# Work from two head pairs on stands in where a head pair's own steps would wait, in the second mixer of a streaming encoder

## The chip, the cores and the metric

The kernel runs on one core of one Trainium2 chip. The metric is the device time of one execution in microseconds (us). A core has five engines with a queue of instructions each, and each works its queue strictly in order: PE (TensorE, matmuls; its weight loads are listed apart as PEld), DVE (VectorE), ACT (ScalarE), POOL (GpSimd) and SP (SyncE, which here only issues DMAs). An instruction that waits for another engine holds up all that stands behind it in its own queue.

## The reference

One inference step of two layers for 1,152 tokens (1,024 of a prompt and 8 streams of 16), with a model width of 1,024. Layer 0 is stick-breaking attention beside a convolution; layer 1 is a banded attention with a learned bias by relative position; each is followed by a squared-ReLU MLP. The change lies in layer 1's mixer:

```python
def c_project(h, w_in):
    B, T, _ = h.shape
    p = (h @ w_in).reshape(B, T, 3, N_C_HEADS, HEAD_DIM)
    return p[:, :, 0], p[:, :, 1], p[:, :, 2]

def band_attention(q, k, v, q_pos, k_pos, rel_bias):
    s = jnp.einsum('bqhd,bkhd->bhqk', q, k).astype(jnp.float32) * (HEAD_DIM ** -0.5)
    rel = jnp.clip(q_pos[:, None] - k_pos[None, :], -REL_CLIP, REL_CLIP) + REL_CLIP
    s = s + rel_bias[:, rel].astype(jnp.float32)
    ...
    p = jax.nn.softmax(jnp.where(mask, s, -jnp.inf), axis=-1)
    return jnp.einsum('bhqk,bkhd->bqhd', p.astype(v.dtype), v)
```

Sixteen heads of 64 are computed; every token sees its own chunk of 64 and the eight chunks before it, with a running cache for the streams.

## The kernel before

All is in 32-bit floats; a factor is split into a high and a low part (`split`, lines 183 to 186: ACT copies the high part, DVE subtracts to get the low one), and a product is three matmuls of them.

**The second mixer** (`mixer1`) goes through eight pairs of heads, p = 0 to 7. For one pair it needs three projections, q, k and v (chunks 3p, 3p + 1 and 3p + 2 of the weights), each for three groups g of 384 tokens. One such sum, of one chunk and one group, is 24 matmuls (`dense`, line 225), which come as two steps of 12; the text calls 12 such matmuls a *block*. A pair has 18 blocks. Their result is in a PSUM bank `psc{p}{n}{g}` (n is 0 for q, 1 for k, 2 for v) until DVE scales it into `sq`, `sk` or `sv` (line 1122). The weights of a chunk come in two halves `hl_wc{chunk}_{half}`: SP loads them to a `st` buffer (three of them), then ACT and DVE split them into one of four `hl` buffers, so that two chunks fit.

The attention of pair p has two heads i and, for each, four jobs t of two query tiles q of 128. A tile's chain is: scores on PE (`zc{p}{i}{q}`, lines 1201 and 1202), the bias and the maximum on DVE (line 1165, in two parts where the tile is wide), the exponential on ACT (line 1168), the scaling on DVE (lines 1169 and 1170) into `s{p}{i}{q}`. For a job, PE then turns the blocks of its two tiles (`tpc{p}{i}{t}{group}`, line 455), ACT and DVE split them (`whc`, `wlc`), PE multiplies with the values (`avc{p}{i}{t}`, line 467), and ACT and DVE finish (`atc`, `cpc`). Beside it run the streams' tokens (`zs`, `zn`, `sn`, `st`, `so`, `sq{p}{bg}`). Before a pair begins, `expand_qk` makes its `q`, `k` and `l` operands on ACT and DVE (lines 348 to 353), and they overwrite those of the pair before.

**What sets the order.** The work of a pair is three lists of steps: `steps` (the attention, with what is carried over from the pair before), `sample` (the streams) and `fill` (the projections of the next pair, 18 blocks). `merge` (lines 53 to 76) lays them into one. It keeps a clock of PE's planned time; a step has a planned PE cost and may have to come a lag after a named step. Among the heads of the lists it takes the one that is ready first, and among those ready the one whose list is least far on. The merged order goes to a framework that queues each engine's instructions and may still let one slip past another on the same engine where it expects a wait. From pair 1 to pair 6 the `fill` list runs out before `steps` does, because the last job's turns and products follow each other with lags. The last job of pair p (i = 1, t = 3) is carried into pair p + 1. Pair 7 has the output projection (`psoa`) as its `fill` and loads `cr` from memory for it. Here *tail of pair p* is the stretch from `tpc{p}12` on, where PE has only steps left that hang on each other.

Of the kernel before, what the change touches and what calls it, by code (L numbers as in the profile page):

```python
# [49 lines left out]
        self.pe, self.go, self.dve, self.name, self.after, self.lag = pe, go, dve, name, after, lag  # L50


def merge(*lists):


    lists = [steps for steps in lists if steps]
    total = [sum(s.pe for s in steps) or 1.0 for steps in lists]
    at, done = [0] * len(lists), [0.0] * len(lists)
    out, now = [], 0.0
    ends = {s.name: 1e9 for steps in lists for s in steps if s.name}  # L60
    while True:
        heads = []
        for n, steps in enumerate(lists):
            if at[n] < len(steps):
                s = steps[at[n]]
                ready = max(now, ends.get(s.after, -1e9) + s.lag)
                heads.append((ready, (done[n] + 0.5 * s.pe) / total[n], n, s))
        if not heads:
            return out
        now, _, n, s = min(heads, key=lambda e: e[:3])  # L70
        out.append(s)
        at[n] += 1
        done[n] += s.pe
        now += s.pe
        if s.name:
            ends[s.name] = now
# [22 lines left out]
def run(steps):  # L99
    for s in steps:  # L100
        s.go()
# [23 lines left out]
def tile_trunk(ctx, tc, ins, outs):  # L125
# [128 lines left out]
    def new_hs(name):  # L254
        return [[new_h(g, half, name) for half in range(2)] for g in range(NG)]
# [54 lines left out]
    def chunk_steps(n, got, ahead, h, ks, evac, name, depth=1, per=12):  # L310

        steps = [Step(0.0, lambda: [ahead(n + d) for d in range(depth + 1)], 1200.0)]
        for g in range(NG):
            box = {}

            def ps(g=g, box=box):
                if "p" not in box:
                    box["p"] = bank(f"ps{name}{g}")
                return box["p"]

            steps += dense(ps, lambda: got[n], h, g, ks, per)
            steps.append(Step(0.0, lambda g=g, ps=ps: evac(ps(), g), 470.0))
        return steps

    def chunks_steps(ns, got, ahead, h, ks, evac, name, depth=1):

        steps = [Step(0.0, lambda: [ahead(n) for n in range(ns[0], ns[-1] + depth + 1)])]
        for g in range(NG):
            for n in ns:
                box = {}  # L330

                def ps(g=g, n=n, box=box):
                    if "p" not in box:
                        box["p"] = bank(f"ps{name}{n}{g}")
                    return box["p"]

                steps += dense(ps, lambda n=n: got[n], h, g, ks)
                steps.append(Step(0.0, lambda n=n, g=g, ps=ps: evac(n, ps(), g), 470.0))
        return steps
# [757 lines left out]
    def mixer1(nx, win):  # L1097
        h, rstd = nx.h, nx.r
        with ExitStack() as st:
# [12 lines left out]
            def staged(p, n, ps, g):  # L1112
                tag = ("sq", "sk", "sv")[n]
                if p == 0 and n < 2:
                    if n == 0:
                        nx.run_rows(g)
                    elif g == 0:
                        nx.end(1)
                        nx.end(2)
                if g == 0:  # L1120
                    S[tag, p] = pp.tile([P, T], F32, tag, f"{tag}1{p}")
                tt(S[tag, p][:, g * G:g * G + G], ps[:, :G], rstd[g], ALU.mult)
                if g == 2 and n:
                    put(outs["c_k" if n == 1 else "c_v"][p], S[tag, p])

            def proj(p):
                if p == 0:
                    return (chunks_steps([0, 1], got, ahead, h, ks, lambda n, ps, g: staged(0, n, ps, g), "c")
                            + [Step(0.0, lambda: expand_qk(0))]
                            + chunk_steps(2, got, ahead, h, ks, lambda ps, g: staged(0, 2, ps, g), "c02"))  # L1130
                steps = []
                for n in range(3):
                    steps += chunk_steps(3 * p + n, got, ahead, h, ks, lambda ps, g, n=n: staged(p, n, ps, g),
                                         f"c{p}{n}")
                return steps

            def expand_qk(p):
                q, k = S["sq", p], S["sk", p]
                expand(qs, kd, kl, q, k)
                S["qn"] = pp.tile([P, P], F32, "qn", f"qn1{p}")  # L1140
                S["kn"] = pp.tile([P, P], F32, "kn", f"kn1{p}")
                ACT(S["qn"], q[:, TP:], AF.Copy, scale=0.125)
                ACT(S["kn"], k[:, TP:], AF.Copy)
# [43 lines left out]
            def attend(p, cat):  # L1187
                def job(i, t):
                    ws = {}

                    def one(q):
                        n = min(q + 1, 5) * P
                        k0 = (q + 1) * P - n
                        b0 = 640 - n
                        s = ep.tile([P, 640], F32, "s", f"s{p}{i}{q}")
                        pieces = []
                        qc = slice(q * P, q * P + P)
                        for c, m in ((0, n),) if n <= 512 else ((0, 384), (384, 256)):
                            z = bank(f"zc{p}{i}{q}{c}")
                            kc = slice(k0 + c, k0 + c + m)  # L1200
                            mm(z[:, :m], qs[i][:, qc], kd[i][:, kc], start=True, stop=False)  # L1201
                            mm(z[:, :m], qs[i][:, qc], kl[i][:, kc], start=False, stop=True)  # L1202
                            pieces.append((z[:, :m], S["bp", p, i][:, b0 + c:b0 + c + m], c, m))
                        softmax(s, pieces, n, f"c{p}{i}{q}")
                        ws[q] = (s, k0)

                    q0, q1 = 2 * t, 2 * t + 1
                    keys = {j: [q for q in (q0, q1) if max(0, q - 4) <= j <= q] for j in range(max(0, q0 - 4), q1 + 1)}
                    blocks = Blocks(keys, lambda j, q: ws[q][0][:, j * P - ws[q][1]:j * P - ws[q][1] + P])

                    def cost(q):
                        return 2 * max(256, min(q + 1, 5) * P) * PASS

                    name = f"c{p}{i}{t}"
                    return (Step(cost(q0), lambda: one(q0), 1100.0), Step(cost(q1), lambda: one(q1), 1100.0, f"z{name}"),
                            split_weigh_steps(vs, wk, cat, i, t, blocks, name, f"z{name}"))

                return [job(i, t) for i in range(2) for t in range(4)]
# [6 lines left out]
                s["w"] = w  # L1225

            run(proj(0))
            carry, cat_t = [], None
            for p in range(8):
                S["p"] = p  # L1230
                if p == 7:
                    cat_t = new_hs("cat1")
                cat = Cat(1, p, wk, cat_t)
                jobs = attend(p, cat)
                s3 = jobs[3][0]
                s3.go = lambda p=p, go=s3.go: (bias_p(p, 1), go())
                body, left = pipeline(jobs[1:], jobs[0][2])
                steps = carry + [jobs[0][0]]
                steps += [Step(327.0, lambda p=p, g=g: expand_v(p, g)) for g in range(NG)]
                if p == 7:  # L1240
                    bias_p(p, 0)
                    expand_qk(p)
                    run(merge(steps, ready_chunks(1, range(3), pp, cat_t)))
                    steps = []
                steps += [jobs[0][1]] + body
                carry = left
                cs = sample_out(cat, wk, p)
                sample = [Step(0.0, lambda p=p: biases(p))]
                load = sample_caches(1, p, cp)
                sample += two_samples(*(sample_steps(1, p, bg, S, wk, load, soft, cs) for bg in range(2)))  # L1250
                back = []
                if p < 7:
                    fill = proj(p + 1)
                else:
                    fill = sum(part_out(1, range(3), pp, cat_t), [])
                    steps += carry
                    back = ready_chunks(1, range(3, 7), pp, cat_t)
                if p < 7:
                    bias_p(p, 0)
                    if p:  # L1260
                        expand_qk(p)
                run(merge(steps, sample, fill, back))
            return cat_t


# [701 lines left out]
```

## Time and profile before

| | us |
|---|---|
| median of three runs | 2751.92 |
| lowest and highest of them | 2749.00, 2752.41 |
| the profiled execution's own time | 2750.03 |
| its span, first to last instruction | 2748.2 |

The profile is of one execution. Its rows give a start in us from the span's start, a duration, the engine, the line, the operation, output<-inputs with the buffers' numbers left out, a count (x12) and, in brackets, the idle time of the engine before it and what ended that. Matmuls overlap each other, so a row of x12 lasts longer than its share of PE's time; the weight loads (PEld) keep step with it. The "releaser" of a wait is inferred. Most of the kernel is outside `mixer1`: its eight pairs take from about 1,333 to 1,946 us.

### The profile page before, as it was taken

What the parts mean: (1) busy time and instruction counts of PE and PEld (TensorE: products, weight loads), DVE (VectorE), ACT (ScalarE), POOL (GpSimd) and SP (SyncE); (2) the same over time, 40 slices, a digit from 0 to 9 for tenths busy, and PEclk for the clock granted to TensorE, in tenths of its full rate; (3) what the DMA queues carried; (4) which work ended last, traced back from release to release, by engine and by line L of the source; (5) the groups of instructions that cost most, each with busy time, mean ns of one, the idle gap of its engine ahead of it and who ended that gap; (6) DMA issues with size and microseconds to landing.
All of it is one profiled execution on the core that took longest, in us unless ns stands there. A gap on an engine that the chain in (4) does not pass through costs nothing.

```text
span 2748.2 us, 50583 instructions
## 1 busy us (share of the span) xinstructions
PE 2669.0 (97%) x19362; PEld 2557.1 (93%) x19362; DVE 2090.5 (76%) x4117; ACT 1389.0 (51%) x2906; POOL 328.3 (12%) x599
## 2 busy tenths in 40 slices
PE   8999898999999999999999999998999999999998
PEld 8987776799999999999999999997999999999998
DVE  8999998888777755758577777778787777647577
ACT  5344456755554543435355555556555555434344
POOL 1100101041111100000011111110221111100001
PEclk9999999999999999999999999999999999999999
DMA  4434446454343377435444444446533343684344
GB/s 157 121 111 147 118 141 223 145 176 143 139 146 141 138 260 250 124 100 170 146 140 138 140 135 135 139 132 229 179 132 137 141 145 138 230 270 134 96 125 145
DMA packets 173203, 422.90 MB, mean 154 GB/s; under 512 B 25968, under 2 KB 53808, under 8 KB 170912
## 3 DMA queue, kind: packets, MB, share of 16 engines
q1 hardware_dynamic: 135696, 288.38, 33.1%
q0 software_dynamic: 37120, 131.27, 13.9%
q8 instruction: 152, 2.49, 0.4%
q14 instruction: 91, 0.75, 0.1%
q10 hardware_dynamic: 144, 0.02, 0.0%
HBM read 289.60 MB, written 117.34 MB: 148 GB/s over the span
## 4 chain that ended last, share of the span: by engine, by line
PE 76%; DVE 12%; ACT 4%; issue 4%; DMA 3%; POOL 0%; SPq 0%; DVEq 0%; ACTq 0%; POOLq 0%
PE um L1461 25%; PE pd L1686 25%; PE psc L225 10%; PE psp L225 3%; DVE y L735 3%; PE avc L467 2%; PE tpc L455 2%; DVE kp L907 2%; PE f L225 1%; PE psoa L225 1%; DMA cr<-cat_d 1%; PE zc L1201 1%; PE zc L1202 1%; PE zs L568 1%; PE so L602 1%
## 5 line engine op out<-in xcount | busy, mean ns | idle before, releaser
L225 PE MATMUL psc<-h,hl_wc 128*128 128x384 f32 x1728 | 327.2, 339 | 0.0
L225 PEld LDWEIGHTS psc<-h,hl_wc 128*128 128x128 f32 x1728 | 296.8, 188 | 13.3 <-issue 10.9
L1461 PE MATMUL um<-sl,hl_m 128*128 128x288 f32 x1548 | 240.3, 295 | 0.0
L1461 PEld LDWEIGHTS um<-sl,hl_m 128*128 128x128 f32 x1548 | 217.7, 188 | 0.0
L1686 PE MATMUL pd<-tm,hl_wd 128*128 128x288 f32 x1584 | 214.7, 294 | 0.0
L1686 PEld LDWEIGHTS pd<-tm,hl_wd 128*128 128x128 f32 x1584 | 211.3, 189 | 0.0
L735 DVE SCALAR_TENSOR_TENSOR y<-u,dw,y 128x1024 f32<-128x1024 f32 (+1 forms) x232 | 177.8, 806 | 0.6
L225 PE MATMUL psp<-h,hl_wi 128*128 128x384 f32 x864 | 165.7, 344 | 0.0
L1468 ACT ACTIVATE hdm<-hdm 128x288 f32<-128x288 f32 x192 | 84.7, 442 | 156.5 <-DVE hdm L1467 154.8
L225 PEld LDWEIGHTS psp<-h,hl_wi 128*128 128x128 f32 x864 | 150.9, 191 | 7.0 <-issue 6.2
L186 DVE TENSOR_TENSOR tm<-xr,tm 128x576 fp32r<-128x576 f32 (+1 forms) x120 | 85.8, 715 | 93.9 <-ACT tm L185 93.6
L185 ACT ACTIVATE tm<-xr 128x576 fp32r<-128x576 f32 (+1 forms) x120 | 77.6, 646 | 95.8 <-PE pd L1686 74.0
L1168 ACT ACTIVATE s<-s,mxc 128x640 f32<-128x640 f32 (+4 forms) x128 | 88.9, 694 | 60.2 <-DVE mxc L1165 58.6
L1461 PE MATMUL um<-sl,hl 128*128 128x288 f32 x756 | 119.1, 296 | 0.0
L1686 PE MATMUL pd<-th,hl_wd 128*128 128x288 f32 x792 | 113.7, 297 | 3.8 <-DVE th L186 3.7
L1686 PEld LDWEIGHTS pd<-th,hl_wd 128*128 128x128 f32 x792 | 108.2, 190 | 4.8 <-DVE th L186 4.2
L1686 PE MATMUL pd<-xr,hl_wd 128*128 128x288 f32 x792 | 112.4, 296 | 0.0
L1686 PEld LDWEIGHTS pd<-xr,hl_wd 128*128 128x128 f32 x792 | 108.0, 190 | 0.0
L1461 PEld LDWEIGHTS um<-sl,hl 128*128 128x128 f32 x756 | 106.4, 188 | 0.8
L1686 PE MATMUL pd<-tm,hl 128*128 128x288 f32 x768 | 104.9, 295 | 0.0
L1686 PEld LDWEIGHTS pd<-tm,hl 128*128 128x128 f32 x768 | 103.1, 188 | 0.0
L185 ACT ACTIVATE whc<-tpc 128x512 fp32r<-128x512 f32 (+1 forms) x144 | 72.5, 523 | 46.7 <-PE tpc L455 45.8
(526 smaller groups left out, 6637.0 us busy)
## 6 DMA issues: line engine op xcount, KB each, us to landing
xr<-hb_d SPq DMA_DIRECT2D x208, 288.0 KB, 3.0
xr<-in_w_up_dram SPq DMA_DIRECT2D x64, 512.0 KB, 4.2
hb_d<-hdm POOLq DMA_DIRECT2D x96, 288.0 KB, 2.4
hb_d<-t POOLq DMA_DIRECT2D x96, 288.0 KB, 2.4
wm<-in_w_down_dram SPq DMA_DIRECT2D x64, 256.0 KB, 4.0
st_wd<-in_w_down_dram SPq DMA_DIRECT2D x64, 256.0 KB, 3.5
st_wc<-in_w_in_c_dram SPq DMA_DIRECT2D x44, 256.0 KB, 2.9
xm_d<-xo POOLq DMA_DIRECT2D x16, 576.0 KB, 3.5
```

The source lines that it names most:

```text
L185: ACT(hi, src, AF.Copy)
L186: return tt(lo, src, f(hi), ALU.subtract)
L225: mm(ps()[:, :G], hl[:, a, at:at + P], act[g][k // 4][b][:, k % 4, :], start=n == 0, stop=n == len(todo) - 1)
L455: nc.tensor.transpose(tp[:, c0 + q * P:c0 + (q + 1) * P], blocks.get(j, tile_q), ident)
L467: mm(st["av"][:, o0:o0 + n], vs[:, j, i].rearrange("p a d -> p (a d)"), src[:, c0:c0 + n], start=st["done"] == 0, stop=st["done"] == nmm - 1)
L568: mm(box["z"][at // 512][own, at % 512:at % 512 + kw], qb[:, own], k[:, b * kw:b * kw + kw], start=True, stop=True)
L735: stt(src if j == CW - 1 else dst, src, wj, dst, ALU.mult, ALU.add)
L907: nc.vector.tensor_tensor_scan(keep[:, 0:n][:, ::-1], keep[:, 0:n][:, ::-1], ones[:, 0:1].to_broadcast([P, n]), 1.0, ALU.mult, ALU.mult)
L1168: ACT(s[:, :n], s[:, :n], AF.Exp, bias=mx, scale=-1.0, accum_out=tot)
L1461: mm(banks[b, n][:, :TQ], w[:, a, c * P:c * P + P], combo(key, c)[:, h, n * TQ:n * TQ + TQ], start=k < 3 and c == 0 and i == 0, stop=c == ...
L1468: ACT(y, y, AF.Relu)
L1686: mm(ps, w[:, a, m * P:m * P + P], b[:, h, (n - ns[0]) * TQ:(n - ns[0]) * TQ + TQ], start=first and s == 0, stop=j == NJ - 1 and s == 2, s ...
```

## The change

`merge` takes one more list, `spare`. Where the earliest head of all lists is still more than 400 ns of planned time away, it puts the next step of `spare` there instead. `mixer1` gives it, for pairs 0 to 5, the first three steps of the projections two pairs on: loading ahead, and the two blocks of `psc{p+2}00`. What was not placed leads the next pair's `fill`, and what was placed is missing from it.

```diff
-def merge(*lists):
+def merge(*lists, spare=()):
...
         if not heads:
             return out
+        if spare and min(heads)[0] > now + 400.0:
+            out.append(spare.pop(0))
+            now += out[-1].pe
+            continue
         now, _, n, s = min(heads, key=lambda e: e[:3])
...
-            carry, cat_t = [], None
+            carry, cat_t, left_over, rest_of = [], None, [], []
...
                 back = []
+                spare = []
                 if p < 7:
-                    fill = proj(p + 1)
+
+                    fill, spare = left_over + (rest_of if p else proj(1)), []
+                    if p < 6:
+                        rest_of = proj(p + 2)
+                        spare, rest_of = rest_of[:3], rest_of[3:]
...
-                run(merge(steps, sample, fill, back))
+                run(merge(steps, sample, fill, back, spare=spare))
+                left_over = spare
```

No instruction of the eight pairs is added or taken away; they change places. In pairs 0 and 1 PE's `fill` still has 18 blocks. Pair 0 places none of its spare. In pairs 1 to 5 both spare blocks are placed, so that the `fill` of pairs 2 to 6 has 16 blocks, and those of pairs 2 to 5 get two more at their tails. Pair 6 has no spare: 16 blocks in all, against 18 before. Counted by pair, two blocks move from each pair 2 to 6 to the one ahead of it; the sum is that pair 1 has two more and pair 6 two fewer. Lines of the changed kernel are up to ten higher (225 is 229, 455 is 459, 467 is 471, 1201 is 1205).

Three places carry the prediction. The first is PE at the tail of pair 1: `sq111` is the last thing before the wait for `whc1120`. Before, with "..." for the rest of the scores and for turns:

```order
L610 MATMUL sq111_16213<-ident_69,sb111_16081 128x128
L467 MATMUL avc112_16220<-whc1120_16200,vs1_14196 128x256 x2
L1201 MATMUL zc1170_16226<-k1_14193,q1_14191 128x384
...
L467 MATMUL avc112_16220<-wlc1120_16201,vs1_14196 128x256 x2
...
L467 MATMUL avc112_16220<-whc1121_16209,vs1_14196 128x256 x2
L467 MATMUL avc112_16220<-wlc1121_16210,vs1_14196 128x256 x2
L455 MATMUL tpc1130_16298<-ident_69,s116_16168 128x128
L225 MATMUL psc300_16307<-h1_00_13863,hl_wc9_0_15924 128x384
```

In the changed kernel, with "..." for the rest of a block (the first) and for scores, turns and products (the second):

```order
L614 MATMUL sq111_16213<-ident_69,sb111_16081 128x128
L229 MATMUL psc300_16230<-h1_00_13863,hl_wc9_0_15924 128x384
...
L229 MATMUL psc300_16230<-h1_30_13975,hl_wc9_0_15924 128x384
L471 MATMUL avc112_16243<-whc1120_16200,vs1_14196 128x256 x2
L471 MATMUL avc112_16243<-wlc1120_16201,vs1_14196 128x256 x2
L1205 MATMUL zc1170_16249<-k1_14193,q1_14191 128x384
...
L471 MATMUL avc112_16243<-wlc1121_16210,vs1_14196 128x256 x2
L229 MATMUL psc300_16230<-h1_40_13712,hl_wc9_1_15929 128x384
```

The first block of `psc300` now stands ahead of the products of `whc1120`, and the second whole behind those of `wlc1121`; before, `psc300` came in pieces behind the first turn of `s116`, 15 of its matmuls ahead of the first turn of `s117`. Now 24 are.

The second is ACT at the tail of pair 2 (pairs 3 to 5 read alike), where PE waits for `whc2120`. Before:

```order
L1168 ACTIVATE s216_17073,totc216_17084<-s216_17073,mxc2161_17082 128x640
L185 ACTIVATE hl_wc13_1_17198<-st_wc13_1_17196 128x512
L185 ACTIVATE whc2120_17105<-tpc2120_17100 128x512
L185 ACTIVATE whc2121_17114<-tpc2121_17109 128x512
L348 ACTIVATE k1_14193<-sk13_16664 64x1024
```

In the changed kernel:

```order
L1172 ACTIVATE s216_17115,totc216_17126<-s216_17115,mxc2161_17124 128x640
L189 ACTIVATE whc2120_17147<-tpc2120_17142 128x512
L189 ACTIVATE whc2121_17156<-tpc2121_17151 128x512
L352 ACTIVATE k1_14193<-sk13_16552 64x1024
L189 ACTIVATE whc2122_17183<-tpc2122_17180 128x256
```

The split of the next weights no longer stands between the exponential of `s216` and `whc2120`. PE's order there has 12 matmuls of `psc400` ahead of `avc211` and 12 ahead of `tpc2120`, where those of `psc322` were, and 19 of `psc401` between `tpc2120` and the turns of `s217`, where 15 of `psc400` were. `sq121` has moved ahead of the first of these.

The third is the tail of pair 6. PE before, with "..." for the rest of a block and for products and scores:

```order
L1202 MATMUL zc615384_20644<-l1_14195,q1_14191 128x256
L225 MATMUL psc722_20656<-h1_00_13863,hl_wc23_0_20139 128x384
...
L225 MATMUL psc722_20656<-h1_30_13975,hl_wc23_0_20139 128x384
L467 MATMUL avc611_20669<-whc6110_20628,vs1_14196 128x256 x2
...
L1202 MATMUL zc616384_20687<-l1_14195,q1_14191 128x256
L225 MATMUL psc722_20656<-h1_40_13712,hl_wc23_1_20144 128x384
...
L225 MATMUL psc722_20656<-h1_70_13826,hl_wc23_1_20144 128x384
L455 MATMUL tpc6120_20710<-ident_69,s614_20608 128x128
L455 MATMUL tpc6120_20710<-ident_69,s615_20640 128x128
```

PE in the changed kernel, with "..." for the rest of the products and scores:

```order
L1206 MATMUL zc615384_20670<-l1_14195,q1_14191 128x256
L614 MATMUL sq161_20681<-ident_69,sb161_20559 128x128
L471 MATMUL avc611_20688<-whc6110_20654,vs1_14196 128x256 x2
L1205 MATMUL zc6160_20703<-k1_14193,q1_14191 128x384
L1206 MATMUL zc6160_20703<-l1_14195,q1_14191 128x384
L471 MATMUL avc611_20688<-wlc6110_20655,vs1_14196 128x256 x2
...
L1206 MATMUL zc616384_20706<-l1_14195,q1_14191 128x256
L459 MATMUL tpc6120_20717<-ident_69,s614_20634 128x128
L459 MATMUL tpc6121_20726<-ident_69,s614_20634 128x128
L459 MATMUL tpc6120_20717<-ident_69,s615_20666 128x128
```

And DVE in the changed kernel at the same place, from the first part of `s615`'s maximum to its scaling, with "..." for small steps of 128x1 ("ISA" is the bias with the maximum; lines 1174, 642 and 481 are 1170, 638 and 477 of the kernel before):

```order
L1169 ISA s615_20666,mxc6150_20673<-zc6150_20667,bp61_20292 128x384
...
L642 COPY cs16_20425<-sq161_20681 64x64
L1174 TENSOR_SCALAR s614_20634<-s614_20634,totc614_20645 128x640
L1169 ISA s615_20666,mxc6151_20675<-zc615384_20670,bp61_20292,mxc6150_20673 128x256
...
L642 COPY cs16_20425<-sq161_20681 64x64
L481 TENSOR_TENSOR cpc611_20699<-avc611_20688,atc611_20697 64x256
L1169 ISA s616_20702,mxc6160_20709<-zc6160_20703,bp61_20292 128x384
...
L1169 ISA s616_20702,mxc6161_20711<-zc616384_20706,bp61_20292,mxc6160_20709 128x256
...
L1174 TENSOR_SCALAR s615_20666<-s615_20666,totc615_20677 128x640
```

Both blocks of `psc722` are gone from here (they stand ahead of `avc610` now), so that `zc615`, `avc611`, `zc616` and the turns of `s614` and `s615` follow each other directly. On DVE the first two parts for `s616` and two copies for `sq161` now come ahead of the scaling of `s615`; before, that scaling was ahead of `s616`.

## The prediction

> **What bounds the kernel now.** The page comes first, for the bound of the whole; then PE's waits in the second mixer; then its tails in order of time.
>
> ```profile
> span 2748.2 us, 50583 instructions
> PE 2669.0 (97%) x19362; PEld 2557.1 (93%) x19362; DVE 2090.5 (76%) x4117; ACT 1389.0 (51%) x2906; POOL 328.3 (12%) x599
> ```
>
> PE is busy in 97% of the span, so a change of order can win idle time of PE and nothing else: 79 us in the whole kernel. Asked for PE's waits from 1430 to 1850 us (pair 0 to the last of pair 6's body), the trace lists two (columns: total, times, longest):
>
> ```profile
> PE avc L467 <- ACT whc L185: 5.7, 5, 1.2
> PE tpc L455 <- DVE s L1170: 2.5, 6, 0.7
> ```
>
> The five and the six are the tails of pairs 1 to 5 (and one of pair 0); in the bodies between them PE waits for nothing. The windows show the pairs one by one (length, busy time of PE, PEld, DVE, ACT, POOL, granted clock, DMA):
>
> ```profile
> 1506.90:1577.02 70.12, 68.56 (x506) 64.58 (x505) 51.76 (x146) 38.04 (x89) 8.97 (x22) 1.00 0.45 137
> 1787.43:1857.57 70.14, 68.56 (x505) 64.59 (x505) 51.41 (x145) 37.48 (x87) 8.86 (x21) 1.00 0.44 132
> 1857.57:1865.10 7.53, 3.14 (x21) 2.65 (x20) 6.91 (x15) 5.52 (x11) 2.19 (x4) 0.92 0.63 181
> 1865.10:1871.00 5.90, 5.75 (x27) 5.35 (x28) 3.51 (x7) 2.91 (x6) 0.82 (x3) 0.53 0.99 267
> ```
>
> The pairs repeat to 0.02 us: 70.1 us, of which PE idles 1.6. So all that the five tails can give is about 5 x 1.5 = 7.5 us, 0.27% of the span. The third row is pair 6's tail, where PE works 3.1 us of 7.5; in the fourth PE runs at a clock of 0.53.
>
> The tail of pair 1, in order of time:
>
> ```profile
> 1503.57 2.04 PEld L225 LDWEIGHTS psc<-h,hl_wc 128*128 128x128 f32 x12
> 1505.93 0.83 ACT L1168 ACTIVATE s<-s,mxc 128x640 f32<-128x640 f32 x1 [1.73 <-DVE mxc L1165]
> 1506.63 0.27 PE L610 MATMUL sq<-ident,sb 128*128 128x128 f32 x1
> 1506.76 0.61 ACT L185 ACTIVATE hl_wc<-st_wc 128x512 fp32r<-128x512 f32 x1
> 1507.40 1.09 ACT L185 ACTIVATE whc<-tpc 128x512 fp32r<-128x512 f32 x2
> 1508.05 0.51 PE L467 MATMUL avc<-whc,vs 128*128 128x256 f32 x2 [1.14 <-ACT whc L185]
> 1508.06 1.29 DVE L186 TENSOR_TENSOR wlc<-tpc,whc 128x512 fp32r<-128x512 f32 x2
> 1509.06 1.06 ACT L348 ACTIVATE k<-sk 64x1024 fp32r<-64x1024 f32 x1 [0.57 <-PE zc L1201]
> 1511.63 0.83 ACT L1168 ACTIVATE s<-s,mxc 128x640 f32<-128x640 f32 x1
> 1513.44 0.55 DVE L1170 TENSOR_SCALAR s<-s,totc 128x640 f32<-128x640 f32 x1
> 1514.05 0.88 PE L455 MATMUL tpc<-ident,s 128*128 128x128 f32 x6 [0.36 <-DVE s L1170]
> ```
>
> Two waits are to be seen: 1.14 us for `whc1120`, which ACT begins only after an exponential and a split of weights, and 0.36 us for `s117`. A block of 12 matmuls takes 2.04 us, 0.17 us each; it is longer than either wait.
>
> **The change, part by part.** No instruction is added; the terms are the waits at six tails.
>
> *Pair 1* gets two blocks that it did not have. The first starts at 1506.90 where PE stopped, and ends at 1508.94, after `whc1120` came (1508.05): the wait of 1.14 goes. By the turns of `s117` PE has now done 24 matmuls of `psc300`, not 15, so it arrives 9 x 0.17 = 1.5 us of work later. `s117` itself moves little: `zc117` ends about 1.1 us later, but its exponential now stands ahead of `q1` on ACT, and the scaling that ended at 1513.99 comes at about 1513.6 to 1514.2. PE's own work to there is the first block's 2.04, the second's 2.04 and the 3.0 us of small matmuls that lie between 1508.05 and 1513.69 beside 15 x 0.17: arrival at about 1514.0. Both waits go: **-1.5 us** (bounds 0, if `s117` slips by as much as its scores, and -1.5).
>
> *Pairs 2 to 5* have the same count of blocks as before, from other chunks. What differs is, on ACT, the 0.61 us split that no longer stands ahead of `whc`: `whc` can start when the exponential ends (1505.93 + 0.83 and a small read, about 1506.9), takes 0.55, and PE goes on at about 1507.5, not 1508.05. Ahead of `s217` stand 19 matmuls and not 15, 4 x 0.17 = 0.7 us that cover the 0.36. On the other side DVE now does `q1` (1.22 us, in the rows below) ahead of the scaling, which takes back what DVE gained from the earlier `whc`. So the turns of `s217` start at the old time, with 0.7 us more of PE's work behind them, less a short new wait for `whc2122`, which now stands ahead of more fill: **-0.5 us each, -2.0 in all** (bounds -1.5 and +0.5 each).
>
> *Pair 6* loses two blocks, 2 x 2.04 = 4.1 us of work. If PE's work bound this tail, it would be 4.1 us shorter, and the term would cancel what pair 1 took on. But it hangs on DVE:
>
> ```profile
> 1850.90 1.15 DVE L186 TENSOR_TENSOR wlc<-tpc,whc 128x512 fp32r<-128x512 f32 x2
> 1851.96 0.55 DVE L1165 CUSTOM_DVE_ANT_0 s<-zc,bp 128x384 f32<-128x384 f32 x1
> 1852.66 0.48 DVE L1165 CUSTOM_DVE_ANT_0 s<-zc,bp,mxc 128x256 f32<-128x256 f32 x1
> 1854.35 2.24 PE L225 MATMUL psc<-h,hl_wc 128*128 128x384 f32 x12
> 1854.59 0.56 DVE L1170 TENSOR_SCALAR s<-s,totc 128x640 f32<-128x640 f32 x1
> 1855.18 0.42 DVE L477 TENSOR_TENSOR cpc<-avc,atc 64x256 f32<-64x256 f32 x1
> 1856.43 1.03 PE L455 MATMUL tpc<-ident,s 128*128 128x128 f32 x8
> 1858.46 0.51 PE L467 MATMUL avc<-whc,vs 128*128 128x256 f32 x2 [0.89 <-ACT whc L185]
> 1859.09 0.21 DVE L638 COPY cs<-sq 64x64 f32<-64x64 f32 x1
> 1860.33 0.56 DVE L1165 CUSTOM_DVE_ANT_0 s<-zc,bp 128x384 f32<-128x384 f32 x1
> 1861.83 1.22 DVE L351 TENSOR_TENSOR l<-sk,k 64x1024 fp32r<-64x1024 f32 x1
> 1863.28 1.22 DVE L353 SCALAR_TENSOR_TENSOR q<-sq,q 64x1024 fp32r<-64x1024 f32 x1
> 1864.53 0.55 DVE L1170 TENSOR_SCALAR s<-s,totc 128x640 f32<-128x640 f32 x1
> 1865.14 1.54 PE L455 MATMUL tpc<-ident,s 128*128 128x128 f32 x6 [3.25 <-DVE s L1170]
> ```
>
> In the new order DVE does, from the end of the `wlc` at 1852.05: first part of `s615` 0.55, scaling of `s614` 0.55, second part 0.48, two copies 0.42, `cpc611` 0.42, the two parts of `s616` 0.55 and 0.48, scaling of `s615` 0.56, and some 0.3 of reciprocals: 4.3 us, `s615` at 1856.4. PE, without the blocks, is at these turns 4.1 us before 1856.43 and waits some 3.5 to 4 us in a new place. From there the gain is small: four turns (half of the row of x8, 0.5 us) and one `whc` (0.55 to 0.6) put `avc612` at about 1857.6 instead of 1858.46, and DVE then has `wlc` twice, the parts of `s617`, `l`, `q`, `wlc`, `cpc` and the scaling, the same as before. The end at 1865.14 comes 0.9 us earlier. Of the 4.1 us of work taken out, 3.2 stay as waiting: **+3.2 us** (bounds +1.0, if DVE follows more closely, and +4.1).
>
> *The clock at pair 6.* In the old trace one wait of 3.25 us was followed by a granted clock of 0.53 for 5.9 us, while waits of 1.14 left it at 1.00. The new wait for `s615` is 3.5 to 4, so I let the clock fall there too. It then lies on the chain: six turns take 1.54 us and not 0.88 (both rows above), and products and scores up to `zc617` lose about 0.5 as well: **+1.2 us** (bounds 0 and 2.7, the latter for PE's 5.75 busy us at 0.53). [...] The trace has a drop after 3.25 us already, so here it takes no longer wait than that.
>
> *Queues.* On SP the bias of the next pair (`bp30` and so on) moves behind two loads of weights, some 30 us ahead of use: nothing. At the start of pair 7 `cr` loads move ahead of a bias; PE's idle time there is 74.00 - 69.63 = 4.4 us in this row:
>
> ```profile
> 1871.00:1945.00 74.00, 69.63 (x497) 63.23 (x496) 61.63 (x182) 42.87 (x109) 4.30 (x8) 1.00 0.60 206
> ```
>
> No step there has a clear side: 0, bounds -1 and +1.
>
> **Sum.** -1.5 - 2.0 + 3.2 + 1.2 = +0.9 us. The profiled execution took 2750.03 us and would take 2750.9; it lies 1.9 below the median of the runs, 2751.92, so the forecast against the median is 2752.8. A measurement of this kernel can tell about 0.2% from no change, 5.5 us: 2746.4 to 2757.4. That is no change.
>
> **The rivals.**
>
> *All five tails lose their waits and pair 6 follows* (faster). For it: in pairs 2 to 5 a split leaves ACT's queue and more fill stands in the second wait. Against it: these pairs get no block more than before. It gives -1.5 for pair 1, -6.0 for the four others, +1.5 for pair 6 with the clock as before: -6.0, so 2745.9. It decides where PE idles under 0.3 us at the tails of pairs 2 to 5. Chance 0.08.
>
> *Pair 6 loses its cover and its clock* (slower). Mechanism: the wait for `s615` trips the clock, PE is too idle after it to get it back, and it stays at half through the wait for `s617` into pair 7. For it: the row at 0.53 after 3.25 us, and 3.1 busy us in the 7.5 before that. Against it: the stretch hangs on DVE and ACT, which keep their speed. It costs the whole cover of 4.1, 1.2 on the chain and 2.7 for a second stretch like that row; with pair 1's -1.5 and nothing from pairs 2 to 5 that is +6.5, so 2758.4. It decides if the clock stays under 0.6 for over 10 us around pair 6's tail. [...] Chance 0.12.
>
> *It does not do what it says*: at pairs 2 to 5 the spare only stands in for the block that is missing from the same place, pair 1's second wait comes back behind the longer fill, and pair 6's tail shortens as PE's work does. Each term is near 0: 2751.9. Chance 0.10.
>
> **How the numbers follow.** The forecast has 0.70, 2752.8. Same is 0.70 + 0.10 = 0.80, faster 0.08, slower 0.12. The range takes pairs 2 to 5 at -1.2 each and pair 6 at +1.0 without the clock term for its low end (-1.5 - 4.8 + 1.0 = -5.3, which leaves the faster rival out), and the slower rival at the other (+6.5); drawn in by 0.8 and 0.5, since not all bounds come together: 2747.4 to 2757.9.
>
> **What would show it.** Right: the window of pair 1's tail has no wait of PE over 0.3 us; those of pairs 2 to 5 keep one for `whc` of 0.5 to 0.9; at pair 6 a new wait of PE for DVE's scaling of 3 us or more stands ahead of `tpc6120`'s turns, with a clock under 0.7 behind it; the bodies of pairs 2 to 6 stay free of waits. Wrong: a period of pairs 2 to 5 that differs from 70.1 by over 1 us, new waits in a body (fewer blocks between scores and turns), or a pair 6 that is 4 us shorter than before.

## The result, and the profile after

| | before | after |
|---|---|---|
| median of 20 runs each, us | 2753.20 | 2756.66 |
| lowest and highest, us | 2747.34, 2757.05 | 2752.02, 2761.49 |
| span of the profiled execution, us | 2748.2 | 2753.7 |

The ratio of after to before is 1.0016, with a 95% interval of 1.0010 to 1.0022: 4.4 us slower (2.8 to 6.1). That is clear of zero, and the interval reaches to both sides of the 0.2% line. The forecast, 2752.8 with a range of 2747.4 to 2757.9, was 0.9 us above before; the measured time lies in the range, 3.9 us above the forecast. Of these 3.9, 1.3 are the kernel before itself, whose median was 2751.92 when the forecast was made and is 2753.20 here.

The page of the changed kernel begins like that of before, with PE at 97% and 6.5 us more busy:

```profile
span 2753.7 us, 50553 instructions
PE 2675.5 (97%) x19362; PEld 2560.4 (93%) x19362; DVE 2089.5 (76%) x4117; ACT 1387.9 (50%) x2906; POOL 329.0 (12%) x599
```

PE's waits from 1430 to 1850 us in the changed kernel (total, times, longest):

```profile
PE avc L471 <- ACT whc L189: 4.0, 4, 1.0
PE tpc L459 <- DVE s L1174: 2.0, 5, 0.7
```

Against 5.7 and 2.5 before, that is 2.2 us less waiting, in a kernel that is slower. The stretch ends ahead of pair 6's tail; over the whole kernel PE's idle time still falls by 1.0 us (79.2 to 78.2). So the waits don't tell where the time went. I cut both traces at one event that every pair has, the last scores of tile 7 (`zc{p}17`), from pair 0 to pair 6, and then to the last product of pair 7. First before:

```profile
1436.76:1508.86 72.10, 70.27 (x519) 66.56 (x517) 53.02 (x149) 38.66 (x89) 9.47 (x22) 1.00 0.47 149
1508.86:1578.97 70.11, 68.56 (x507) 64.58 (x506) 51.75 (x146) 38.03 (x88) 9.50 (x22) 1.00 0.45 137
1578.97:1649.12 70.15, 68.59 (x507) 64.60 (x506) 51.78 (x146) 38.03 (x88) 8.97 (x22) 1.00 0.46 137
1789.39:1859.28 69.89, 68.57 (x508) 64.59 (x506) 50.95 (x144) 37.61 (x88) 8.41 (x20) 1.00 0.43 126
1859.28:1945.25 85.97, 77.95 (x542) 70.67 (x540) 70.82 (x201) 49.80 (x122) 6.74 (x14) 0.96 0.64 212
```

and the changed kernel, where two rows like the third are left out in both:

```profile
1436.34:1509.35 73.01, 72.32 (x532) 68.86 (x531) 53.93 (x150) 38.67 (x89) 10.05 (x23) 1.00 0.49 150
1509.35:1580.89 71.54, 70.51 (x517) 66.71 (x516) 51.19 (x146) 37.91 (x88) 8.98 (x21) 1.00 0.46 139
1580.89:1651.54 70.65, 69.16 (x507) 64.75 (x506) 51.43 (x146) 37.95 (x88) 8.88 (x21) 1.00 0.45 136
1792.90:1863.38 70.48, 66.94 (x483) 61.73 (x482) 51.47 (x146) 37.62 (x88) 8.86 (x21) 0.97 0.43 131
1863.38:1951.29 87.91, 82.23 (x540) 74.02 (x540) 69.44 (x197) 49.15 (x121) 6.19 (x13) 0.93 0.62 197
```

The first two stretches hold pair 1's tail: +0.9 and +1.4 us, where two blocks of 2.04 us more are worked. Each stretch between pairs 2 and 5 has the same 507 matmuls and is 0.5 us longer, while PE's idle time in it *fell* (70.15 - 68.59 = 1.56, 70.65 - 69.16 = 1.49). The stretch to pair 6 has two blocks fewer, and is 0.6 us longer. Pair 7 is 1.9 us longer. Together +6.5 us; at the start of the first stretch the two executions were 0.4 us apart the other way, and the rest after pair 7 was 0.6 shorter, which leaves the 5.5 between the spans.

**Pair 1's tail** is as forecast: no wait of PE ahead of `whc1120`'s products (1508.41) or of the turns of `s117` (1512.81).

```profile
1506.24 2.33 PE L229 MATMUL psc<-h,hl_wc 128*128 128x384 f32 x12
1508.41 0.40 PE L471 MATMUL avc<-whc,vs 128*128 128x256 f32 x2
...
1510.18 2.25 PE L229 MATMUL psc<-h,hl_wc 128*128 128x384 f32 x12
...
1512.81 1.17 PE L459 MATMUL tpc<-ident,s 128*128 128x128 f32 x8
```

**The tail of pair 4**, first before (turns, exponential, the split of weights, `whc`, its first products), then in the changed kernel:

```profile
1716.14 1.04 PE L455 MATMUL tpc<-ident,s 128*128 128x128 f32 x8
1716.31 0.83 ACT L1168 ACTIVATE s<-s,mxc 128x640 f32<-128x640 f32 x1 [1.73 <-DVE mxc L1165]
1717.14 0.61 ACT L185 ACTIVATE hl_wc<-st_wc 128x512 fp32r<-128x512 f32 x1
1717.78 1.09 ACT L185 ACTIVATE whc<-tpc 128x512 fp32r<-128x512 f32 x2
1718.43 0.50 PE L467 MATMUL avc<-whc,vs 128*128 128x256 f32 x2 [1.14 <-ACT whc L185]
```

```profile
1719.34 1.08 PE L459 MATMUL tpc<-ident,s 128*128 128x128 f32 x8
1719.81 0.83 ACT L1172 ACTIVATE s<-s,mxc 128x640 f32<-128x640 f32 x1 [1.47 <-DVE mxc L1169]
1720.76 1.09 ACT L189 ACTIVATE whc<-tpc 128x512 fp32r<-128x512 f32 x2
1721.40 0.51 PE L471 MATMUL avc<-whc,vs 128*128 128x256 f32 x2 [0.99 <-ACT whc L189]
```

The split is gone from ACT's queue and the wait is still 0.99 us. Counted from the first turn, the exponential now begins 0.47 us later and not 0.17, held up by its maximum on DVE, and `sq`, 0.27 us of PE, no longer stands in front of the wait. The weight loads (PEld) show three small waits in that pair, at the carried job and the streams; the last two are new, the first was 0.36 before but has one matmul less ahead of it:

```profile
1653.26 0.30 PEld L471 LDWEIGHTS avc<-whc,vs 128*128 128x128 f32 x2 [0.35 <-ACT whc L189]
...
1659.47 0.30 PEld L471 LDWEIGHTS avc<-wlc,vs 128*128 128x128 f32 x2 [0.24 <-DVE wlc L190]
...
1665.88 0.30 PEld L577 LDWEIGHTS zn<-kn,qb 128*128 128x128 f32 x2 [0.24 <-DVE cpc L481]
```

**Pair 6's tail** has the new wait for `s615` that was forecast, of 2.31 us after one of 0.48, then 2.04 for `s617`; each time the six turns behind it take 1.54 us, not 0.88:

```profile
1857.57 0.41 PE L459 MATMUL tpc<-ident,s 128*128 128x128 f32 x2 [0.48 <-DVE s L1174]
1860.29 1.54 PE L459 MATMUL tpc<-ident,s 128*128 128x128 f32 x6 [2.31 <-DVE s L1174]
...
1869.33 1.54 PE L459 MATMUL tpc<-ident,s 128*128 128x128 f32 x6 [2.04 <-DVE s L1174]
```

**Pair 7** was forecast at nothing. Its first `zs` is four products on 32 columns each (a product of this kernel shows as two records, so x8 is all four). Before they stood together; in the changed kernel they come as one, one and two, between output projections:

```profile
1873.70 1.06 PE L568 MATMUL zs<-ct17k,qb 128*32 128x512 f32 x8
```

```profile
1878.49 1.04 PE L572 MATMUL zs<-ct17k,qb 128*32 128x512 f32 x2
...
1881.15 1.04 PE L572 MATMUL zs<-ct17k,qb 128*32 128x512 f32 x2
...
1882.68 1.05 PE L572 MATMUL zs<-ct17k,qb 128*32 128x512 f32 x4
```

One, two or four take about the same: 1.04, 1.05 and 1.06 us. From start to start a part holds PE for 0.97 us (1878.49 to 1879.46 at the next matmul), so two more parts are 1.9 us of PE's time. Pair 7 is 1.9 us longer, but that it is these 1.9 us is not shown, because the stretch differs as much between kernels whose PE order there is the same by its tile names. The old order took 85.97 us (before), 88.18, 86.66 and 85.18 (experiments 2, 6 and 8 below); the new one took 87.91 (the changed kernel), 87.05, 86.60 and 86.45 (experiments 1, 4 and 7). The means are 0.5 us apart. The two ends of the old order are:

```profile
1864.71:1952.89 88.18, 78.57 (x542) 70.48 (x540) 70.88 (x201) 49.81 (x122) 6.74 (x14) 0.96 0.63 206
1859.66:1944.84 85.18, 78.43 (x542) 70.75 (x540) 70.46 (x199) 49.85 (x122) 6.35 (x14) 0.96 0.65 214
```

The changed kernel's execution also has a stretch at half the clock there with PE busy throughout, which none of the other seven has at that place:

```profile
1916.95:1920.37 3.42, 3.42 (x23) 3.17 (x25) 3.42 (x11) 0.64 (x3) 0.53 (x1) 0.50 0.63 224
```

The 43 records of `psoa` (9) and `so` (34) that it falls on take 4.42 us from start to start (1916.69 to 1921.11), and as many of the same shapes take 2.88 before, at a clock of 1.00 (1909.21 to 1912.09): 1.5 us more.

### The profile page after: what moved, and what is told of

It reads as the page before. It is cut to its first block, busy times and chain, and to the rows that moved or that the text cites. A ratio compares the mean times of both kernels' runs of the same rounds, so it can differ in the third digit from the quotient of the medians.

```text
span 2753.7 us, 50553 instructions
## 1 busy us (share of the span) xinstructions
PE 2675.5 (97%) x19362; PEld 2560.4 (93%) x19362; DVE 2089.5 (76%) x4117; ACT 1387.9 (50%) x2906; POOL 329.0 (12%) x599
## 4 chain that ended last, share of the span: by engine, by line
PE 76%; DVE 13%; issue 4%; ACT 3%; DMA 3%; POOL 0%; SPq 0%; DVEq 0%; ACTq 0%; POOLq 0%
PE pd L1696 26%; PE um L1471 25%; PE psc L229 10%; PE psp L229 3%; DVE y L739 3%; PE avc L471 2%; DVE kp L911 2%; PE tpc L459 2%; PE f L229 1%; PE psoa L229 1%; PE zc L1205 1%; PE zs L572 1%; PE zc L1206 1%; DVE sg L913 1%; PE so L606 1%
```

## The experiments

The theory at the start: the ends (pair 1's gain, pair 6's bare tail, pair 7) and the new order at pairs 2 to 5 cost separately. The rivals: all of it sits at pair 6, or all in the repeated tails. "Us against before" is the ratio's middle and interval times 2751.

**1. Only pair 5 gets blocks.**

```
+                    if p == 5:
                         spare, rest_of = rest_of[:3], rest_of[3:]
```

> Only pair 5 gets two blocks of pair 7's projections; pairs 1 to 4 keep the old order, pair 6 is left with 16 blocks. Theory A (the ends and the repeated tails both cost: pair 5's covered tail gains 1.8 us, the 4.1 us of blocks taken from pair 6 save nothing there, pair 7 starts 1.3 later, and the rest of the change's loss, 0.5 us for each of pairs 2 to 5, needs their new order): periods of pairs 2 to 4 are 70.1, the total is 2.3 to 3.6 us above before. Rival B (all of the loss sits in pair 6 and behind it): the total is 4.4 to 5.5 us above before, as with the whole change. Rival C (all of the loss is repeated in the tails): within 1 us of before.

Measured: 1.0002 (0.9994 to 1.0011), 0.6 us (-1.7 to 3.0). Cut as above, pairs 1 to 4 have the old periods (70.11 to 70.15). Up to pair 6's last scores it has lost 2.0 us, pair 7 is 1.1 longer (its `zs` is in three parts here too). Pair 6's waits are those of the whole change, 2.31 and 2.04. The repeated loss needs the order of pairs 2 to 5, as in A; all of it at pair 6 (B) is out. The middle of the total lies below A's 2.3 to 3.6 and inside C's 1 us; the interval reaches into both and does not part them.

**2. Only pair 1 gets blocks**: the same line with `p == 1`.

> Only pair 1 gets two blocks; pair 2 is left with 16 and pairs 3 to 6 keep the old order, so that the bare tail stands where a full pair follows. Theory A: pair 1's tail gains 1.8 us as in the whole change, pair 2's tail saves nothing of its 4.1 us, the rest is as before: 2.0 to 2.5 us above before, with a wait of 2 us or more ahead of the turns at pair 2's tail. Rival B (the bare tail costs only beside pair 7's start): pair 2's tail is 3 us or more shorter and the total 1 to 2 us below before. Rival D (the clock falls at pair 2's tail and stays low): over 4 us above before, granted clock under 0.6 there for over 5 us.

Measured: 1.0010 (1.0001 to 1.0018), 2.8 us (0.3 to 5.0). Pair 2's bare tail waits 0.77, 2.20 and 0.42 us. Up to pair 6 it loses 2.5 us: the 4.1 of pair 1's blocks, less about 1.7 of waits, and what pair 2 was relieved of is all given back within its tail and the first scores behind. Theory A holds up to there; a bare tail saves nothing even where a full pair follows. The granted clock falls to a mean of 0.89 over the 7.6 us of the tail and 0.89 over the 7.9 us behind it.

**3. The order without the crossing.** Each of pairs 1 to 6 holds back its own last two blocks.

```
-                    fill, spare = left_over + (rest_of if p else proj(1)), []
...
+                    fill = proj(p + 1)
+                    if p:
+                        fill, spare = fill[:-3], fill[-3:]
...
-                left_over = spare
+                run(spare)
```

> Each of pairs 1 to 6 holds back the last two blocks of its own projections for the waits; nothing crosses from pair to pair, every pair keeps 18 blocks. PE's order at the tails of pairs 2 to 5 is that of the whole change, with other chunks, sq moved ahead as there. Theory A (the moved order costs 0.5 us a pair): periods of pairs 2 to 5 are 70.5 to 70.7, the total 2.5 to 3.2 us above before. Rival B: periods 70.1, total within 0.7 us of before.

Measured: 1.0009 (1.0000 to 1.0017), 2.5 us; periods 70.80 to 70.85, somewhat over A's 70.5 to 70.7. PE's waits over three pairs (pair 2's last scores to pair 5's):

```profile
PE avc L471 <- ACT whc L189: 4.1, 3, 1.4
PE tpc L459 <- DVE s L1174: 1.0, 3, 0.4
```

No block is moved between pairs, and each pair loses 0.7 us. So a loss of this kind needs only the order, not the crossing. The split of weights is back in ACT's queue here, and the wait is 1.38 against 0.99 in the whole change, 0.39 more beside a split of 0.61 us.

**4. The copies on DVE.** The whole change, `sq` held until 2700 ns of planned time after the scores of job t = 2 (`f"zc{p}12"`, in place of `f"o{name}{nz - 1}"`, 1200), which puts it behind the scores of tile 6.

> The whole change, but sq of the second half of the streams is held behind the last scores of tile 6, so that its two copies on DVE stand behind that tile's first maximum. Theory A1 (the 0.5 us a pair come from these copies ahead of the maximum, which hold up exp and whc): periods of pairs 2 to 5 fall from 70.65 to 70.2 or less, the wait for whc at their tails falls from 0.99 to 0.5 or less, and the total is 1.5 to 2.5 us below the whole change's. Rival A2 (they come from the thinner fill behind the turns, with its waits for whc2122, wlc2131 and zn): periods stay at 70.6 and the total stays within 0.7 us of the whole change's.

Measured: 1.0016 (1.0007 to 1.0024); periods 70.77 to 70.80, wait for `whc` 1.09. A1 falls as the main cause: with the copies behind the first part of tile 6's maximum the exponential still begins 0.53 us after the first turn (1719.42 against 1718.89), no sooner than in the whole change. The copies are not wholly out of the way, since one still stands between the two parts (at 1718.78; the second part starts 0.13 us later, at 1718.91), but that is too little for A1's 0.5 us. A2 is not refuted; no run takes its waits away.

**5. One own block, only for planned waits over 1600 ns.** As in 3, with `fill[:-2], fill[-2:]` and `now + 1600.0`.

> Each of pairs 1 to 6 holds back one block of its own projections, and the planner may use it only where its clock sees a wait of over 1600 ns, so that its matmuls stand behind the first turns of tile 5's and the rest of the turns, directly ahead of the products of whc. Nothing crosses pairs. Theory P (where a block stands decides, not how many there are: a block directly in the wait for whc takes its 1.14 us, as at pair 1 of the whole change): periods of pairs 2 to 5 are 69.0 to 69.5, no wait of PE for whc over 0.3 at the tails, total 4 to 7 us below before. Rival Q (the tail hangs on DVE, so that the wait moves to the turns of tile 5, which now have one block less ahead of them): periods 69.9 or more, a wait for DVE's scaling of 0.8 us or more ahead of those turns, total within 2 us of before.

Measured: 1.0039 (1.0025 to 1.0054), 10.7 us *slower*. The stretch of three pairs (length, then busy PE) and what became of `zs` (the second fence is in order of time):

```profile
1578.28:1790.75 212.47, 210.66 (x1518) 194.52 (x1516) 154.82 (x436) 112.96 (x265) 26.81 (x63) 1.00 0.43 136
```

```profile
1586.88 1.05 PE L572 MATMUL zs<-ct13k,qb 128*32 128x512 f32 x2
1587.86 0.50 PE L471 MATMUL avc<-wlc,vs 128*128 128x256 f32 x2
1588.29 1.06 PE L572 MATMUL zs<-ct13k,qb 128*32 128x512 f32 x6
```

Both theories fall. The block does stand in the wait for `whc`, and PE idles only 0.6 us a pair (212.47 - 210.66 = 1.8 in three). But the period is 70.8. One of a pair's two `zs` has come apart into one and three, and both parts last as long as the whole. Pair 7 of the changed kernel has the same kind of parting. The pairs hold only a part of the total: in the profiled execution pairs 1 to 6 lost 3.3 us together and pair 7 lost 3.9 (89.89 us). Why the middle of the runs is higher still is not shown.

**6. The same block, for waits over 400 ns.**

> The same held-back block, but the planner may use it in any planned wait over 400 ns; it then stands ahead of the turns, where a block stood before the change already. Theory P: the wait for whc stays at 0.9 or more and the periods at 70.1 to 70.8, total 0 to 4 us above before. Rival Q' (holding back a block helps wherever it is put): as the kernel with 1600 ns.

Measured: 1.0012 (1.0003 to 1.0020), 3.3 us; periods 70.67 to 70.69; wait for `whc` 1.11. As P: where the block stood already, it wins nothing, and each pair is 0.5 us longer than before.

**7. The whole change with 1600 for 400 ns.**

> The whole change with 1600 in place of 400 ns. Pair 1's and pair 6's orders stay much as in the whole change; at pairs 2 to 5 the two blocks leave the places ahead of the turns: 14 matmuls stand between the turns of tiles 4 and 5, 2 ahead of the products of whc. Theory P: the products of whc get more time behind the turns of tile 5 no more than 0.3 us, but the maxima and exponentials ahead of them lose 4 us of cover, so the periods stay at 70.3 to 71.2 and the total at 3 to 7 us above before. Rival (the threshold alone makes the change slow): periods 69.5 or less, total below before.

Measured: 1.0034 (1.0022 to 1.0046), 9.4 us; periods 71.19, with 0.77 us of waiting between the turns of tiles 4 and 5. The periods are P's, at the upper edge; the total is above what I gave it. The threshold alone is not what makes the change slow.

**8. As 3, with `sq` held back as in 4.**

> Each pair's own last two blocks held back (as in the kernel with periods of 70.8), and sq of the streams' second half held behind the scores of tile 6, so that its copies on DVE stand behind the second maximum of that tile. Theory D (the tail's end is a chain through DVE, which the copies, 0.43 us, hold up): the wait for whc falls from 1.38 to 1.0 or less and the periods to 70.3 to 70.5. Rival E (the copies only take idle time of DVE, the loss is the thinner fill): periods 70.7 or more, wait for whc 1.25 or more.

Measured: 1.0011 (1.0002 to 1.0019), 3.0 us; periods 70.52 to 70.55; wait for `whc` 1.12. Here both copies stand behind the whole maximum of tile 6, and the wait for `whc` is 0.26 us shorter than in 3 (1.38 to 1.12), the period 0.28. D is half right, and 0.4 us a pair stay with `sq` out of the way. Between 8 and 4, too, the split of weights is there in one and not in the other, and the waits are 1.12 and 1.09: 0.03 apart here, 0.39 between 3 and the whole change. DVE's order differs in both comparisons as well, so neither figure is the price of the split.

**9. `zs` by itself.** The kernel before, with the four products as two steps.

```
-                + [Step(1300.0 * nz / nk, lambda c=c: keys(c), 0.0, None, f"q{name}", 3000) ...
+                   [Step(650.0, lambda: keys(0, (0,)), 0.0, f"k{name}", f"q{name}", 3000),
+                    Step(650.0, lambda: keys(0, (1, 2, 3)), 0.0, None, f"k{name}", 2500)]),
```

> The kernel before, with the four 128x32 products of each zs of the second mixer in two parts, one and three, with other matmuls between; PE's order is otherwise the old one in pairs 1 to 6. Theory S (the four run side by side, 0.006 us apart, and a part of them takes as long as all four, 0.98 us): two more parts in each pair, so periods rise from 70.1 to 71.9 to 72.1 and the total by 14 to 16 us. Rival (the parts share the time, or the split is hidden in idle time of PE): periods 70.1 to 70.6, total within 4 us of before.

Measured: 1.0056 (1.0043 to 1.0069), 15.4 us. Three pairs, and the two parts of one `zs`:

```profile
1589.26:1806.39 217.13, 212.45 (x1517) 194.28 (x1516) 155.29 (x436) 114.04 (x264) 26.94 (x64) 1.00 0.44 133
```

```profile
1669.70 1.05 PE L570 MATMUL zs<-ct14k,qb 128*32 128x512 f32 x2
...
1673.63 1.06 PE L570 MATMUL zs<-ct14k,qb 128*32 128x512 f32 x6
```

217.13 / 3 = 72.38 a pair, +2.25 for two more parts, of which 1.9 are the parts by their 0.97 us each; the rest is not traced. S holds, with a period 0.3 above what it gave; of the orders tried here this is the dearest.

**10. The whole change, pair 7's `zs` whole.** The lag 3000 becomes `6000 if layer and p == 7 else 3000`.

> The whole change, with the first zs of pair 7 started a planned 3 us later, so that its four products stand together again, as before the change, and not in three parts; pairs 1 to 6 have the order of the whole change. Theory S: pair 7 is 1.5 to 2.0 us shorter than in the whole change, the total 1.5 to 2 us below it, 2 to 3 us above before. Rival (pair 7's 1.9 us are the late tail of pair 6, or differ from run to run): the total within 0.7 us of the whole change.

Measured: 1.0002 (0.9991 to 1.0014), 0.6 us above before (-2.5 to 3.9), where the whole change is 4.4 above (2.8 to 6.1). Pairs 1 to 6 repeat the whole change's periods (70.66 to 70.69), and pair 7 is:

```profile
1866.49:1948.35 81.86, 76.45 (x540) 70.35 (x540) 69.90 (x197) 49.02 (x121) 6.47 (x13) 0.96 0.64 212
```

81.86 and not 87.91. That is 6.0, more than S's 1.5 to 2: moving `zs` also moved its neighbours, and 81.86 is below each of the four stretches in the old order too (85.18 to 88.18). So this run does not give the price of the parts. Of the 6.0, two parts would be 1.9; the clock could be up to about 2.9 (an estimate from the rows, 0.07 of 87.91 against 0.04 of 81.86); the rest is order.

**11. As 5, with the streams' keys at 2500, so that `zs` stays whole.**

> Each of pairs 1 to 6 holds back one block for waits of over 1600 ns, as in the run with periods of 70.83, and the streams' keys may come 0.5 us of planned time earlier, so that zs stays in one part and stands ahead of the turns of tile 7. Theory S + P (the block in the wait for whc gains 1.4 us a pair, which the split zs took back with 1.07 and later waits with the rest): periods 69.3 to 69.8, pair 7 back at 74, total 2 to 6 us below before. Rival (the gain is lost behind in any case, to the waits for wlc and s): periods 70.0 or more, total at before or above.

Measured: 0.9995 (0.9985 to 1.0005), -1.4 us. Three pairs:

```profile
1580.44:1789.34 208.90, 207.25 (x1518) 193.64 (x1516) 155.18 (x436) 112.94 (x264) 26.92 (x63) 1.00 0.43 138
```

69.63 a pair, 0.5 below before and 1.2 below 5: S and P together give the periods that they said. The total misses them: pair 7 takes 89.9 us there, with a wait of 2.17 for `whc`. Its order is that of 5, where it took 89.89; probably it is pair 6's held-back block that draws other turns forward into it.

**12. What paid, together.** As 11 for pairs 1 to 5, with `8000 if p == 7 else 2500` for the lag.

> What paid, put together: pairs 1 to 5 hold back one block of their own for waits of over 1600 ns, with the streams' keys at 2.5 us of planned time; pair 6 keeps its 18 blocks and its old tail; the first zs of pair 7 comes a planned 5 us later, whole. One zs, at the start of pair 6, is still in parts of one and three. Theory: periods of pairs 2 to 5 are 69.6 to 69.7 (-0.5 each), pair 6 costs 1 us more for the parted zs, pair 7 is 2 to 4 us shorter than before (from the last scores of pair 6 to the last product of pair 7: 82 to 84 and not 86), total 3.5 to 6.5 us below before. Rival (pair 7's gain was the luck of one execution): 85 to 88 there, total 0.5 to 2.5 us below before.

Measured: 0.9986 (0.9977 to 0.9995), 3.9 us faster than before (1.4 to 6.3), and so faster than both kernels. Pairs 2 to 5 (one row of three), pair 6, pair 7:

```profile
1580.77:1789.62 208.85, 207.18 (x1518) 193.60 (x1516) 155.12 (x436) 112.95 (x265) 26.91 (x63) 1.00 0.43 138
```

```profile
1789.62:1860.74 71.12, 69.74 (x505) 64.52 (x504) 51.32 (x145) 37.58 (x88) 8.96 (x21) 1.00 0.40 129
1860.74:1944.21 83.47, 77.47 (x541) 70.85 (x540) 70.69 (x201) 49.90 (x122) 6.73 (x14) 0.96 0.66 218
```

-0.5 a pair, +1.2 for pair 6 with its parted `zs`, -2.5 for pair 7, as expected. Pair 7's 83.47 is one execution, but it lies below each of the four in the old order.

## Why the prediction was right and where it was wrong

- *Pair 1, -1.5*: right. Two blocks of 4.1 us in all made the two stretches 2.3 us longer: -1.7. (The second stretch also holds the first half of pair 2's tail.)
- *Pairs 2 to 5, -0.5 each, -2.0 in all*: **the step that failed**. It was +0.5 each, +2.1 in all, the end of the bounds that I had given (+0.5). I let the 0.61 us of the split count on the path to `whc`, and let 19 matmuls for 15 cover the second wait. The wait for `whc` fell by 0.15 only (1.14 to 0.99), that for `s217` by 0.03 (0.36 to 0.33): the maximum ahead of the exponential came 0.3 later, and `sq`'s cover was gone. On the other side came the new waits for `wlc` and in front of `zn`, 0.24 each as the weight loads show them, and the longer one for `whc2122`; from PE's start to start these three are 0.21, 0.20 and 0.13 more. I had named the last ("a short new wait for `whc2122`") and priced it inside the term. Less the 0.18 won, these rows hold about two thirds of the 0.53; the rest lies in steps of under 0.1 us that no row names. Experiment 3 shows a like loss (0.7) from order alone, with no block moved between pairs, 4 that `sq`'s copies are not the main cause there, 8 that they can be 0.28 us a pair in a neighbouring order. Which move makes which part stays open.
- *Pair 6, +3.2, and its clock, +1.2*: right as a mechanism. The cover was lost, the new wait for DVE stood where it was put, of 2.31 and 0.48 and not 3.5 to 4, and the clock fell behind it. Counted as in the forecast (pair 1's 4.1 of work against pair 6's), the stretches up to pair 6's last scores lost 4.5 in all; less -1.7 and +2.1 that leaves +4.1 for the forecast's 4.4. Experiment 2 shows a bare tail saving nothing elsewhere. How much of it is the clock stays open: in the execution of experiment 1 the six turns behind the same wait of 2.31 took 0.88 us, at the full clock, and the products behind them then waited 0.42 for `whc`.
- *Queues and pair 7, 0 (bounds -1 and +1)*: +1.9 in the profiled executions, outside the bounds, **with the cause open**. The forecast went by queues and loads there and not by PE's order: a `zs` of four products side by side had come apart in three. Experiment 9 shows that two more parts cost 2.25 us in a full pair. In pair 7 their 1.9 us cannot be told from what the stretch varies by with one order (85.18 to 88.18), nor from the 3.4 us at half the clock.
- *The sum*, +0.9, came to 4.4 (2.8 to 6.1) over runs and 5.5 in the profiled pair: 4.1 from the second point and 1.9 from the fourth, less small ones. "No change" held only just, and in part by luck: the term of pairs 2 to 5 had the wrong sign, and its error of 4.1 us fitted into a range of about 5 us to either side.
- *The bound*, that a change of order can win idle time of PE and nothing else, did not hold either. With the same matmuls busy PE rose by 6.5 us; what a row counts as busy also holds a lower clock (six turns in 1.54 us, not 0.88), parted groups (0.97 us of PE for each part) and waits of the weight loads (0.24 us at 1659.47, where PE shows no wait).
- Of the marks that I had set, pair 1's window, a `whc` wait at pairs 2 to 5 (0.99, somewhat over 0.5 to 0.9) and the drop of clock came; the wait of 3 us in one piece did not, and a period over 1 us off did not. The marks asked for waits, and most of the loss was not in waits.

## What to carry to other kernels

Measure a change of order by the distance between two events that both kernels have, before looking at idle time: here PE waited 2.2 us less in five pairs and the kernel was slower. Price a stretch from one execution only where it repeats: pairs 2 to 5 repeat to 0.1 us, pair 7 differs by 3 us with one order. Fill helps only in a wait that really ends last, and fill taken from a later stretch comes back as waiting there. When a planner or scheduler moves work, look whether it takes apart matmuls that run side by side: here the four of a `zs` took 1.06 us together and one alone 1.04.

## What the runs showed of the hardware

- Four fp32 products with 32 columns of weights and 512 of data run side by side: in the `zs` of before at 1873.70 the starts of four records are 0.006 to 0.007 us apart, and the next four follow after 0.43. The x8 of the group lasts 1.06 us there, the x2 and x6 of its parts 1.05 and 1.06 in experiment 9, so a part lasted as long as the group. What makes up a part's 0.97 us of PE's time no run here shows.
- The clock fell inside a wait of 2.31 us, shorter than the 3.25 of before. In the changed kernel the row of that wait has a mean granted clock (the column ahead of the last two) of 0.70:

```profile
1858.00:1860.30 2.30, 0.01 (x1) 0.01 (x1) 2.10 (x8) 1.28 (x3) 0.95 (x2) 0.70 0.00 0
```

In windows of 0.1 us the clock is 1.00 up to 1858.90, 0.62 in the next and 0.50 from 1859.00, about 0.9 us into the wait, which began at 1857.98. Executions with the same order and waits there differ. In the changed kernel, and in the run of experiment 10, the granted clock behind that wait was

```profile
1860.30:1866.00 5.70, 5.59 (x24) 5.13 (x24) 3.88 (x8) 3.95 (x7) 0.66 (x2) 0.52 0.09 23
```

```profile
1863.40:1869.10 5.70, 5.01 (x24) 4.24 (x24) 3.88 (x8) 3.96 (x7) 0.68 (x2) 0.70 0.08 23
```

In experiment 10 the clock was still 1.00 over the wait itself (1861.10 to 1863.40). In the changed kernel a wait of 0.48 us, 0.41 us of turns and about 0.9 of the 2.31 us stood ahead of the drop. What sets its point no run here shows. So a tail of several short waits did not keep the clock here, though none of them was as long as the 3.25 us of before.
